# Projecting the values of two head pairs in one call, and moving one small load to another queue

## The chip, the cores and the metric

The kernel runs on one core of a Trainium2 chip. The metric is device microseconds of one execution. A core has engines with instruction streams of their own: PE (TensorE, matrix products), DVE (VectorE), ACT (ScalarE), POOL (GpSimd) and SP (SyncE, which here only issues DMA transfers). Each stream is executed in order; streams wait for one another by semaphores.

## The reference

One decoder layer over 1024 positions of width 1024, in float32:

```
h = rms_norm(x, norm_mix)
xa, ga, q, f, v, g, m_a, m_b = split(h @ w_in)       # eight groups of 1024 columns
y_a = rg_lru(conv(xa)) * gelu(ga)
y_b = rms_norm(hgrn2(silu(q), f, v)) * silu(g)       # 8 heads of 128
x = x + (sigmoid(m_a) * y_a + sigmoid(m_b) * y_b) @ w_out
x = x + relu(rms_norm(x, norm_mlp) @ w_up)**2 @ w_down
out = rms_norm(x, norm_final)
```

The change touches only how `v`, the group of values, is computed from `h`, and how the weights of the first norm (`norm_mix`, a "gain") come in.

## The kernel before

**Precision.** Every float32 matrix is split into a high and a low part in a reduced format: ACT copies the high part (`wH`, `hT0H`), DVE subtracts it to get the low part (`wL`, `hT0L`). `mm3` (lines 113 to 117) then issues three matmuls, one line each: 115 (high times low), 116 (high times high), 117 (low times high). So every product of a 128x128 stationary block with a moving tile is three matmuls.

**Halves and pairs.** The sequence is worked in two halves of 512 positions (`c` = 0, 1). In a half, the eight heads are worked as four pairs (`p` = 0..3), 256 columns of each group at a time. For a pair the program order is: `project_v`, then `project` of xa, convolution, q, f, the RG-LRU (`rg_lru`, products `pr` and `pi`), the HGRN2 recurrence (`hgrn`), and the gates with the projections g, mb, ga, ma (`gates`), which end with transposes `poT`, and with DVE and ACT work on `g`, `sma` and `y` (the tail of the gates). After the four pairs of the first half, `out_proj` multiplies by `w_out`, and `first_norm(1)` for the second half is done between the two column halves of it. The output product of the second half, the second norm and the MLP follow.

**project and project_v.** `project` keeps a block of weights stationary and moves 512 positions of the normed, transposed input `hT`: 48 matmuls of 512 columns for two banks. `project_v` needs the values with positions on the partitions, so it does the reverse: a 128-position block of `hT` is stationary, and weights move, 256 columns (one pair). For each of four row tiles `tt` it issues 8 blocks `k` times three matmuls, 96 in all, and ACT copies each bank into the tile `v` (line 293).

**Weights.** They come as tiles of 128x1024 in the order of the list `seq`, over SP's queue (`load_w`, line 84) into four `raw` buffers. `split_w` makes the high and low parts in a pool of six buffers, so three weight tiles are held at a time; `get_w` prepares up to two tiles ahead of the one in use, and a new one needs the buffers of the tile three before it.

**PSUM banks.** The projections, `project_v` and `out_proj` share four banks (tag `pj`); the transposes use two others (tag `hg`).

**The start.** `first_norm(0)` loads four row tiles of `x` and the first three weight tiles by SP's queue, and the gain (128 rows of 4 KB, the same row for every partition) by ACT's queue (line 130). For each row tile: ACT squares and sums (line 136), DVE and POOL make the reciprocal root, DVE scales (line 139), PE transposes (`xT_x`, line 145), ACT and DVE split the result into `hT0H` and `hT0L`.

**What sets the order.** The programs of the engines are written by a scheduler that follows priorities and its own estimate of when inputs are ready, so instructions of neighbouring steps may be interleaved. In the first norm the order of ACT, DVE and POOL is fixed to that of the program text (`keep`).

Of the kernel before, what the change touches and what calls it, by code (L numbers as in the profile page):

```python
# [18 lines left out]
P = 128  # L19
D = 1024  # L20
# [3 lines left out]
NPAIR = 4  # L24
# [1 line left out]
F_MIN = 1e-30  # L26
GELU_C = 0.7978845608028654
GROUPS = {"xa": 0, "ga": 1, "q": 2, "f": 3, "v": 4, "g": 5, "ma": 6, "mb": 7}
ORDER = ("v", "xa", "q", "f", "rg", "g", "mb", "ga", "ma")
N_PAIR_TILES = 17  # L30
MIX_TILES = NPAIR * N_PAIR_TILES
OUT_TILES = 8
QUADS = 16
LEVELS = (2, 8)

# [6 lines left out]
def trunk(ctx: ExitStack, tc: tile.TileContext, x, wts, mlp, pv, gains, mask_f, mask_u, out):  # L42
    nc = tc.nc
    V, A, G, PE = nc.vector, nc.scalar, nc.gpsimd, nc.tensor
# [13 lines left out]
    def bank(tag, name):  # L58
        return ps.tile([P, 512], F32, tag=tag, name=name, bufs={"pj": 4, "sc": 2, "hg": 2}[tag])


    seq = []
    for c in range(NC):
        seq += list(range(MIX_TILES + OUT_TILES))
    seq += list(range(MIX_TILES, MIX_TILES + OUT_TILES))
    ready, made = {}, [0]

# [41 lines left out]
    def next_w():  # L109
        used[0] += 1  # L110
        return get_w(used[0] - 1)

    def mm3(o, ah, al, bh, bl, first, last, goes_on=False):
        how = {"skip_group_check": True} if goes_on else {}
        PE.matmul(o, ah, bl, start=first, stop=False, **how)  # L115
        PE.matmul(o, ah, bh, start=False, stop=False, **how)  # L116
        PE.matmul(o, al, bh, start=False, stop=last, **how)  # L117
# [7 lines left out]
    mhalf = const.tile([P, 8], F32, tag="mhalf", name="mhalf")  # L125
    G.memset(mhalf, -0.5)

    def gain_tile(i):
        g = const.tile([P, D], F32, tag="gain", name=f"gain{i}", bufs=1)
        nc.scalar.dma_start(g, gains[i : i + 1, :].to_broadcast([P, D]))  # L130
        return g


# [20 lines left out]
    def kt(set_, k):  # L154
        return set_[0][k // 4][:, k % 4, :], set_[1][k // 4][:, k % 4, :]
# [9 lines left out]
    gain0 = []  # L165
# [4 lines left out]
    def mt(tag, name, shape=(P, T), dt=F32, bufs=1):  # L170
        return m.tile(list(shape), dt, tag=tag, name=name, bufs=bufs)
# [59 lines left out]
    hT = []  # L231
# [3 lines left out]
    def first_norm(c):  # L235
        dst = a2_set(a2h, f"hT{c}")
        xts = []
        for tt in range(4):
            r = c * 4 + tt
            xt = mt(X_TAGS[tt], f"x{r}", (P, D)) if c == 0 else tile_x(f"x{r}")  # L240
            nc.sync.dma_start(xt, x[r * P : (r + 1) * P, :])
            xts.append(xt)
            if c == 0 and tt == 0:
                gain0.append(gain_tile(0))
            if c == 0 and tt < 3:
                raws.append(load_w(seq[tt]))
        xns = {}

        def rows(tt):
            xns[tt] = mt("f" if tt % 2 == 0 else "tmp", f"xn{c}{tt}", (P, D))  # L250
            norm_rows(xts[tt], xns[tt], gain0[0], f"x{c}{tt}")

        def weights(n):
            if c == 0:
                fill_w(n)

        rows(0)
        weights(1)
        transposed(xns[0], dst, 0, f"x{c}0")
        rows(1)  # L260
        weights(2)
        for tt in range(1, 4):
            if tt < 3:
                rows(tt + 1)
            transposed(xns[tt], dst, tt, f"x{c}{tt}")
        weights(3)
        in_order[0] = False
        hT.append(dst)
# [10 lines left out]
                    mm3(pp[s], wh[:, cols], wl[:, cols], hh, hl, half == 0 and k == 0, half == 1 and k == 3)  # L279
        return pp  # L280

    def project_v(c, name):
        v = mt("v", f"v_{name}", (P, 4, 256))
        w = [next_w(), next_w()]
        for tt in range(4):
            pp = bank("pj", f"pv_{name}_{tt}")
            for k in range(8):
                hh, hl = kt(hT[c], k)
                cut = slice(tt * P, (tt + 1) * P)
                cols = slice((k % 4) * 256, (k % 4 + 1) * 256)  # L290
                wh, wl = w[k // 4]
                mm3(pp[:, :256], hh[:, cut], hl[:, cut], wh[:, cols], wl[:, cols], k == 0, k == 7)
            A.copy(v[:, tt, :], pp[:, :256])
        return v

    def conv(c, p, pp):
# [84 lines left out]
    def hgrn(c, p, q1, f, kk, v):  # L381
# [43 lines left out]
        for li, cw in enumerate(LEVELS):  # L425
            g = 256 // cw
# [8 lines left out]
            for d, a in ((1, 0), (2, 3), (3, 5)):  # L435
                w = (4 - d) * cw
# [39 lines left out]
        for n in range(8):  # L476
            for b in (0, 2):
                k = 4 * n + b
# [42 lines left out]
        for s in range(2):  # L521
            u = 2 * p + s
            pk = bank("hg", f"pk{c}{u}")
            for n in range(nkv):
                PE.transpose(pk[:, n * P : (n + 1) * P], kk[:, s * T + n * P : s * T + (n + 1) * P], ident)
            kT = mt("kT", f"kT{c}{u}", (P, 4, P))
            A.copy(kT[:, :nkv, :], pk[:, : nkv * P].rearrange("p (n k) -> p n k", n=nkv))
            pkv = bank("hg", f"pkv{c}{u}")
            vn = lambda n: v[:, n, s * P : (s + 1) * P]
            for n in range(nkv):  # L530
                PE.matmul(pkv[:, n * P : (n + 1) * P], kT[:, n, :], vn(n), start=True, stop=True)
            sn = mt("sn", f"sn{c}{u}", (P, 3, P))
            state = lambda n: scar[:, u, :] if n in (0, 4) else sn[:, n - 1, :]
            po = bank("hg", f"po{c}{u}")
            for n in range(4):
                only = c == 0 and n == 0
                on_ps = po[:, n * P : (n + 1) * P]
                PE.matmul(on_ps, scT[:, 4 * s + n, :], vn(n), start=True, stop=only)
                if not only:
                    at = s * T + n * P  # L540
                    PE.matmul(on_ps, qf[:, at : at + P], state(n), start=False, stop=True)  # L541
                if n < nkv:
                    kv = pkv[:, n * P : (n + 1) * P]
                    if only:
                        V.tensor_copy(state(1), kv)
                    else:
                        V.scalar_tensor_tensor(
                            state(n + 1), state(n), t128[:, 4 * s + n : 4 * s + n + 1], kv, op0=ALU.mult, op1=ALU.add
                        )
            for n in range(4):  # L550
                A.activation(  # L551
                    on[:, 4 * s + n, :], po[:, n * P : (n + 1) * P], AF.Square, accum_out=ssq[:, 4 * s + n : 4 * s + n + 1]
                )
            A.copy(on[:, 4 * s : 4 * s + 4, :], po.rearrange("p (n d) -> p n d", n=4))
# [71 lines left out]
    for c in range(NC):  # L626
        if c == 0:
            first_norm(0)
            mu32 = small_inputs()
        else:  # L630
            out_proj(0, ys, res0, done0, lambda: first_norm(1))
        ys = a2_set(a2y, f"y{c}")
        for p in range(NPAIR):
            v = project_v(c, f"{c}{p}")
            px = project(c, f"xa{c}{p}")
            if c == 0 and p == 0:
                parameters()
                tc.keep_in_program_order(V.tensor_copy(mu, mu32.to_broadcast([P, 7, 8, 32])))
            xc3 = conv(c, p, px)
            q1 = q_of(c, p, project(c, f"q{c}{p}"))  # L640
            f, kk = f_of(c, p, project(c, f"f{c}{p}"))
            with tc.high_priority(300):
                h = rg_lru(c, p, *xc3)
            on = hgrn(c, p, q1, f, kk, v)
            gates(c, p, h, on, ys)
# [68 lines left out]
    for part in range(2):  # L714
# [5 lines left out]
        for hf in range(2):  # L720
            pp = {tt: bank("pj", f"po1{hf}{tt}") for tt in tts}
            for j in range(4):
                wh, wl = next_w()
                for k in range(2):
                    ku = 2 * j + k
                    yh, yl = kt(ys, ku)
                    cols = slice(k * 512, (k + 1) * 512)
                    for tt in tts:
                        cut = slice(tt * P, (tt + 1) * P)
                        mm3(pp[tt], yh[:, cut], yl[:, cut], wh[:, cols], wl[:, cols], ku == 0, ku == 7)  # L730
            for tt in tts:
                cols = slice(hf * 512, (hf + 1) * 512)
# [16 lines left out]
    def quad_steps(i, pools, raws=raw_tile):  # L749
# [42 lines left out]
        (q, g): dram.tile([P, 2 * len(g) * T], F32, tag=f"u{q}{g[0]}", name=f"u{q}{g[0]}")  # L792
        for q in range(QUADS - 2)
        for g in U_GROUPS
# [59 lines left out]
    work[0]["b"]()  # L854
    for q in range(QUADS):
        n = q + 1 if q + 1 < QUADS else QUADS + QUADS - 2
        if n > 1:
# [78 lines left out]
    for kb in range(n_kb):  # L936
        last = kb + 1 == n_kb
        qs = order[2 * kb : 2 * kb + 2]
        for half in range(2):
# [8 lines left out]
            for step, (bk, wo, uo), prs in [  # L948
                (i, plan, prs) for prs in ([(pr,) for pr in pairs] if alone else [pairs]) for i, plan in enumerate(PLAN)
            ]:  # L950
                for pr in prs:
# [3 lines left out]
                    cut = slice(pr * P, (pr + 1) * P)  # L955
                    for i, q in enumerate(qs):
                        wh, wl = ops_w[QUADS + q][wo]
                        uh, ul = u_ops[q][uo]
                        mm3(banks[bk, pr], uh[:, cut], ul[:, cut], wh, wl, first and i == 0, i == 1, not first)
                for pr in prs:  # L960
                    _, ci, cj, op = ADDS[step]
# [22 lines left out]
def _weights(w_in, w_r, w_i, w_out):  # L984
    tiles = []
    win = _pairs(w_in)
    for p in range(NPAIR):
        for name in ORDER:
            if name == "rg":
                r = np.concatenate([w_r[p].reshape(2, P, 256), w_i[p].reshape(2, P, 256)])  # L990
                tiles.append(r.transpose(1, 0, 2).reshape(1, P, 1024))
            else:
                tiles.append(win[GROUPS[name] * 4 + p])
    wo = w_out.reshape(4, 2, P, 2, 512).transpose(3, 0, 2, 1, 4)
    tiles.append(wo.reshape(8, P, 1024))
    return np.ascontiguousarray(np.concatenate(tiles))


# [50 lines left out]
```

## Time and profile before

| | |
|---|---|
| three runs | 1618.15, 1622.5, 1622.98 us; median 1622.5 |
| the profiled execution's own time | 1617.3 us |
| its span, first to last instruction | 1615.5 us |
| PE busy | 1571.4 us, 97% of the span, 9240 matmuls |
| DVE / ACT / POOL busy | 1210.2 / 761.5 / 63.8 us |
| granted TensorE clock | 0.996 of full speed |

The page of the profile gives busy times for each engine, the chain of work that ended last, and groups of instructions. Rows of the timeline read: start in microseconds from the span's start, duration, engine, line, operation, output and inputs, partitions and columns, and in brackets how long the engine sat idle before and what it waited for. Durations of matmuls overlap: the next one starts before the last has ended, so the pace of PE is read from start to start.

### The profile page before, as it was taken

To read this page: it belongs to the slowest core of one execution; us is meant where nothing else is said; L and a number is where in the kernel's file an instruction comes from. 1 tells how busy PE (TensorE), PEld (TensorE's weight loads), DVE (VectorE), ACT (ScalarE), POOL (GpSimd) and SP (SyncE) were. 2 spreads that over 40 slices of the span, in tenths; PEclk is the share of its full clock that TensorE was granted. 3 is DMA by queue.
4 is the path that set the end of the run, shared out by engine and by line. 5 is a ranking of instruction groups with operands and counts; after the bars stand their busy time and mean duration, and the time that the engine had idled before them with its cause. 6 is when DMAs were issued, how large, how long until landed. Compare 5 with 4: busy or idle time off the path is not lost.

```text
span 1615.5 us, 23190 instructions
## 1 busy us (share of the span) xinstructions
PE 1571.4 (97%) x9240; PEld 1303.4 (81%) x9240; DVE 1210.2 (75%) x1751; ACT 761.5 (47%) x1186; POOL 63.8 (4%) x99
## 2 busy tenths in 40 slices
PE   7999999999999999999999997999999999999998
PEld 6788788788788788788787876888888878888886
DVE  5975966848763865947758688888888888888876
ACT  4643445436432544446345476677667732122113
POOL 0010000100100000000100000000000000000000
PEclk9999999999999999999999998999999999999999
DMA  6212223222243222222222272666666575666652
GB/s 238 92 66 92 92 66 99 72 92 92 79 167 134 92 66 91 92 68 100 69 92 92 95 245 79 258 245 240 247 258 237 229 279 210 258 258 244 258 218 104
DMA packets 57996, 246.51 MB, mean 153 GB/s; under 512 B 6688, under 2 KB 6816, under 8 KB 47136
## 3 DMA queue, kind: packets, MB, share of 16 engines
q1 hardware_dynamic: 56304, 239.27, 40.5%
q10 hardware_dynamic: 1584, 5.77, 1.0%
q8 instruction: 72, 1.18, 0.3%
q14 instruction: 36, 0.29, 0.1%
HBM read 185.24 MB, written 59.77 MB: 152 GB/s over the span
## 4 chain that ended last, share of the span: by engine, by line
PE 81%; DVE 15%; DMA 1%; issue 1%; ACT 1%; POOL 0%; DVEq 0%; POOLq 0%; SPq 0%
PE dX L115 3%; PE dX L116 3%; PE dX L117 3%; PE uX L115 3%; PE uX L117 3%; PE uX L116 3%; DVE wL L77 2%; PE pj_ga L117 2%; PE pj_ga L116 2%; PE pj_ga L115 2%; PE pj_ma L116 2%; PE pj_ma L117 2%; PE pv L115 2%; PE pv L117 2%; PE pv L116 2%; PE pj_ma L115 2%
## 5 line engine op out<-in xcount | busy, mean ns | idle before, releaser
L77 DVE TENSOR_TENSOR wL<-raw,wH 128x1024 fp32r<-128x1024 f32 x160 | 194.5, 1215 | 151.5 <-ACT wH L76 148.7
L76 ACT CAST wH<-raw 128x1024 fp32r<-128x1024 f32 x160 | 167.9, 1049 | 165.9 <-issue 67.2
L963 DVE TENSOR_TENSOR acc<-acc,dX 128x512 f32<-128x512 f32 x128 | 86.9, 684 | 27.6 <-PE dX L117 27.3
L76 ACT CAST wA<-q 128x512 fp32r<-128x512 f32 x32 | 19.8, 621 | 130.7 <-PE dX L117 80.9
L963 DVE TENSOR_TENSOR acc<-acc,dY 128x512 f32<-128x512 f32 x64 | 43.4, 685 | 14.0 <-PE dY L117 12.8
L345 DVE RECIPROCAL rr<-rr 128x512 f32<-128x512 f32 x16 | 53.5, 3346 | 0.0
L823 ACT ACTIVATE b<-b 128x512 f32<-128x512 f32 x48 | 30.2, 630 | 35.8 <-DVE b L822 35.8
L115 PE MATMUL pv<-wL,hT0H 128*128 128x256 f32 x128 | 37.3, 292 | 0.0
L117 PE MATMUL pv<-wH,hT0L 128*128 128x256 f32 x128 | 37.0, 289 | 0.0
L116 PE MATMUL pv<-wH,hT0H 128*128 128x256 f32 x128 | 36.9, 288 | 0.0
L115 PE MATMUL pv<-wL,hT1H 128*128 128x256 f32 x128 | 36.5, 285 | 0.0
L117 PE MATMUL pv<-wH,hT1L 128*128 128x256 f32 x128 | 36.2, 283 | 0.0
L116 PE MATMUL pv<-wH,hT1H 128*128 128x256 f32 x128 | 36.2, 283 | 0.0
L311 DVE SCALAR_TENSOR_TENSOR xc<-xp,pvt,xc 128x512 f32<-128x512 f32 x48 | 33.1, 747 | 0.0
L551 ACT ACTIVATE on<-po 128x128 f32<-128x128 f32 x64 | 16.9, 278 | 33.5 <-PE po L541 33.2
L570 ACT ACTIVATE smb<-pj_mb 128x512 f32<-128x512 f32 x16 | 9.6, 597 | 45.3 <-PE pj_mb L117 45.1
L824 ACT ACTIVATE b<-b 128x512 f32<-128x512 f32 x48 | 30.0, 630 | 1.1
L565 ACT ACTIVATE g<-pj_g 128x512 f32<-128x512 f32 x16 | 9.6, 599 | 37.3 <-PE pj_g L117 37.3
L384 DVE TENSOR_TENSOR seg<-seg 128x128 f32<-128x128 f32 (+2 forms) x96 | 26.8, 309 | 0.2
L444 POOL TENSOR_SCALAR seg<-seg 128x128 f32<-128x128 f32 (+1 forms) x16 | 12.6, 790 | 360.2 <-DVE seg L384 360.2
L117 PE MATMUL pj_ga<-hT1H,wL 128*128 128x512 f32 x64 | 26.5, 414 | 0.0
L384 DVE TENSOR_TENSOR kk<-kk,seg 128x768 f32<-128x768 f32 (+1 forms) x32 | 26.2, 819 | 0.3 <-DVE dd L438 0.3
(1854 smaller groups left out, 5245.8 us busy)
## 6 DMA issues: line engine op xcount, KB each, us to landing
raw<-wts_in SPq DMA_DIRECT2D x160, 512.0 KB, 3.4
q<-mlp_in SPq DMA_DIRECT2D x64, 512.0 KB, 4.0
x<-x_in SPq DMA_DIRECT2D x8, 512.0 KB, 5.9
acc<-x ACTq DMA_DIRECT2D x8, 512.0 KB, 5.4
y_out<-acc SPq DMA_DIRECT2D x16, 256.0 KB, 2.0
xs<-x_in SPq DMA_DIRECT2D x8, 256.0 KB, 4.3
x<-xs SPq DMA_DIRECT2D x8, 256.0 KB, 2.2
x2s<-x_in SPq DMA_DIRECT2D x4, 512.0 KB, 4.5
```

The source lines that it names most:

```text
L76: keep(A.copy(h, src))
L77: keep(V.tensor_tensor(out=lo, in0=src, in1=h.bitcast(F32), op=ALU.subtract))
L115: PE.matmul(o, ah, bl, start=first, stop=False, **how)
L116: PE.matmul(o, ah, bh, start=False, stop=False, **how)
L117: PE.matmul(o, al, bh, start=False, stop=last, **how)
L311: V.scalar_tensor_tensor(xc[:, s, :], xp[:, j : j + T], pvt[:, PV_CW + 8 * j + u : PV_CW + 8 * j + u + 1], xc[:, s, :], op0=ALU.mult, op1= ...
L345: V.reciprocal(rec, rec)
L384: mul = lambda o, a, b: V.tensor_tensor(out=o, in0=a, in1=b, op=ALU.mult)
L551: A.activation(on[:, 4 * s + n, :], po[:, n * P : (n + 1) * P], AF.Square, accum_out=ssq[:, 4 * s + n : 4 * s + n + 1])
L823: A.activation(b[:, at, :], b[:, at, :], AF.Relu, scale=-1.0 if at == 2 else 1.0)
L824: A.activation(b[:, at, :], b[:, at, :], AF.Square)
L963: V.tensor_tensor(out=dst, in0=dst, in1=banks[bk, pr], op=op)
```

## The change

Values are projected once for two pairs. The value weights leave the order of a pair (17 tiles become 15) and are packed anew: four tiles for the first two pairs and four for the last two, each with two blocks `k` of 512 columns. `seq` puts four of them ahead of pairs 0 and 2 of each half. `project_v` is called for even pairs only. It moves 512 columns and holds all four `pj` banks at once: weight tile by weight tile, and in each all four row tiles. For the very first call (`by_rows`), the first three weight tiles are taken together, and each row tile goes through these three before the next row tile, in the program text; the fourth weight tile comes after. The tile `v` is 512 columns wide instead of 256, and `hgrn` picks its quarter of it. The gain of the first norm is loaded by SP's queue, directly behind the first row tile of `x`, instead of ACT's.

```diff
-ORDER = ("v", "xa", "q", "f", "rg", "g", "mb", "ga", "ma")
-N_PAIR_TILES = 17
+ORDER = ("xa", "q", "f", "rg", "g", "mb", "ga", "ma")
+N_PAIR_TILES = 15
+V_TILES = 4
...
     for c in range(NC):
-        seq += list(range(MIX_TILES + OUT_TILES))
+        for p in range(NPAIR):
+            if p % 2 == 0:
+                at = MIX_TILES + OUT_TILES + p // 2 * V_TILES
+                seq += list(range(at, at + V_TILES))
+            seq += list(range(p * N_PAIR_TILES, (p + 1) * N_PAIR_TILES))
+        seq += list(range(MIX_TILES, MIX_TILES + OUT_TILES))
     seq += list(range(MIX_TILES, MIX_TILES + OUT_TILES))
...
-    def gain_tile(i):
+    def gain_tile(i, queue=nc.scalar):
         g = const.tile([P, D], F32, tag="gain", name=f"gain{i}", bufs=1)
-        nc.scalar.dma_start(g, gains[i : i + 1, :].to_broadcast([P, D]))
+        queue.dma_start(g, gains[i : i + 1, :].to_broadcast([P, D]))
         return g
...
             if c == 0 and tt == 0:
-                gain0.append(gain_tile(0))
+                gain0.append(gain_tile(0, nc.sync))
...
-    def project_v(c, name):
-        v = mt("v", f"v_{name}", (P, 4, 256))
-        w = [next_w(), next_w()]
+    def project_v(c, name, by_rows):
+        v = mt("v", f"v_{name}", (P, 4, 512))
+        pp = [bank("pj", f"pv_{name}_{tt}") for tt in range(4)]
+
+        def product(tt, j, w):
+            cut = slice(tt * P, (tt + 1) * P)
+            for k in (2 * j, 2 * j + 1):
+                hh, hl = kt(hT[c], k)
+                cols = slice(k % 2 * 512, (k % 2 + 1) * 512)
+                mm3(pp[tt], hh[:, cut], hl[:, cut], w[0][:, cols], w[1][:, cols], k == 0, k == 7)
+
+        early = 3 if by_rows else 0
+        w = [next_w() for _ in range(early)]
         for tt in range(4):
-            pp = bank("pj", f"pv_{name}_{tt}")
-            for k in range(8):
-                hh, hl = kt(hT[c], k)
-                cut = slice(tt * P, (tt + 1) * P)
-                cols = slice((k % 4) * 256, (k % 4 + 1) * 256)
-                wh, wl = w[k // 4]
-                mm3(pp[:, :256], hh[:, cut], hl[:, cut], wh[:, cols], wl[:, cols], k == 0, k == 7)
-            A.copy(v[:, tt, :], pp[:, :256])
+            for j in range(early):
+                product(tt, j, w[j])
+        for j in range(early, V_TILES):
+            w = next_w()
+            for tt in range(4):
+                product(tt, j, w)
+        for tt in range(4):
+            A.copy(v[:, tt, :], pp[tt])
         return v
...
-            vn = lambda n: v[:, n, s * P : (s + 1) * P]
+            vn = lambda n: v[:, n, (u % 4) * P : (u % 4 + 1) * P]
...
-            v = project_v(c, f"{c}{p}")
+            if p % 2 == 0:
+                v = project_v(c, f"{c}{p}", c == 0 and p == 0)
...
+    at = GROUPS["v"] * 1024
+    wv = w_in[:, at : at + 1024].reshape(4, 2, P, 2, 512).transpose(3, 0, 2, 1, 4)
+    tiles.append(wv.reshape(8, P, 1024))
```

How the scheduler orders it is seen at three places. (In the names, a weight tile carries its number in the packed weights: the eight new value tiles are 68 to 75; `pv_00_2` is half 0, pair 0, row tile 2, followed by the buffer's own number.)

First, the head of SP's queue, before:

```order
L241 DMA x_110<-x_in 128x1024
L84 DMA raw_114<-wts_in 128x1024
L241 DMA x_116<-x_in 128x1024
L84 DMA raw_118<-wts_in 128x1024
L241 DMA x_120<-x_in 128x1024
L84 DMA raw_122<-wts_in 128x1024
L241 DMA x_124<-x_in 128x1024
```

and of the change:

```order
L247 DMA x_110<-x_in 128x1024
L136 DMA gain_112<-gains_in 128x1024
L90 DMA raw_114<-wts_in 128x1024
L247 DMA x_116<-x_in 128x1024
L90 DMA raw_118<-wts_in 128x1024
L247 DMA x_120<-x_in 128x1024
L90 DMA raw_122<-wts_in 128x1024
L247 DMA x_124<-x_in 128x1024
```

The gain stands second in SP's queue; before, it was the first transfer of ACT's. All else keeps its order.

Second, PE in the first call of the change, where the products with the third weight tile (70) begin; 36 value matmuls and all 32 transposes of the first norm stand ahead of them:

```order
L121 MATMUL pv_00_2_229<-wL69_157,hT0H0_106 128x512
L122 MATMUL pv_00_2_229<-wH69_156,hT0H0_106 128x512
L123 MATMUL pv_00_2_229<-wH69_156,hT0L0_108 128x512
L121 MATMUL pv_00_0_227<-wL70_215,hT0H1_107 128x512
L122 MATMUL pv_00_0_227<-wH70_214,hT0H1_107 128x512
L123 MATMUL pv_00_0_227<-wH70_214,hT0L1_109 128x512
```

Row tiles 0, 1 and 2 first take weight tiles 68 and 69, and tile 70 only then; row tile 3 takes all three afterwards, and the 24 products with tile 71 come last. From the first product with tile 70 to the end of the call, 60 matmuls are left.

Third, PE in the change at the first call of the second half, behind `out_proj`; 18 value matmuls stand ahead of these rows:

```order
L121 MATMUL pv_10_1_4206<-wL69_4157,hT1H0_3968 128x512
L122 MATMUL pv_10_1_4206<-wH69_4156,hT1H0_3968 128x512
L123 MATMUL pv_10_1_4206<-wH69_4156,hT1L0_3970 128x512
L121 MATMUL pv_10_2_4207<-wL68_4127,hT1H0_3968 128x512
L122 MATMUL pv_10_2_4207<-wH68_4126,hT1H0_3968 128x512
L123 MATMUL pv_10_2_4207<-wH68_4126,hT1L0_3970 128x512
```

Row tiles 0 and 1 run ahead with weight tile 69, so that the first matmul of row tile 2 is the 22nd of the call, and that of row tile 3 the 32nd. Before, row tiles 2 and 3 began with the 49th and the 73rd matmul of 256 columns.

Elsewhere the streams of DVE, ACT and PE keep their order, with weight tiles renumbered; behind the second half's mixer DVE and ACT have the same instructions and waits in the same order.

## The prediction

> **What bounds the kernel now.** I read the page first (busy times), then PE's waits, then windows by stage, and at last the timeline where the change acts.
>
> ```profile
> PE 1571.4 (97%) x9240; PEld 1303.4 (81%) x9240; DVE 1210.2 (75%) x1751; ACT 761.5 (47%) x1186; POOL 63.8 (4%) x99
> PE xT_x L145 <- DVE xn L139: 10.3, 2, 9.4
> PE sc L394 <- DVE qb L384: 5.0, 8, 0.6
> 126.17:233.50 107.33, 105.92 (x759) 88.92 (x757) 75.50 (x115) 49.87 (x83) 7.70 (x11) 1.00 0.25 84
> ```
>
> The first row is from the page, the next two are PE's waits (total us, times, longest), the last is a window over exactly one head pair (length; PE, PEld, DVE, ACT, POOL busy; granted clock; DMA share; GB/s). PE is busy 105.92 of 107.33 us of a pair, DVE 75.50. So a pair lasts as long as PE's matmuls take to issue, and a matmul removed from it shortens the run. PE's one long wait is that for the first normed rows, 9.4 us at the start.
>
> **The matmuls: 768 of 256 columns become 384 of 512.** Busy times of overlapping matmuls don't give a price, so I go from start to start. The first two rows are the second and the last matmul of one call of `project_v`, the last two stand 16 triples apart in `out_proj`, whose form is that of the new call: a 128-position block stationary, 512 weight columns moving.
>
> ```profile
> 126.38 0.28 PE L116 MATMUL pv<-wH,hT0H 128*128 128x256 f32 x1
> ...
> 137.65 0.28 PE L117 MATMUL pv<-wH,hT0L 128*128 128x256 f32 x1
> ...
> 483.43 0.39 PE L115 MATMUL po<-wL,y0H 128*128 128x512 f32 x1
> ...
> 494.31 0.39 PE L115 MATMUL po<-wL,y0H 128*128 128x512 f32 x1
> ```
>
> 256 columns: (137.65 - 126.38) / 94 = 0.1199 us. 512 columns: (494.31 - 483.43) / 48 = 0.2267 us. Two short ones take 0.2398 us, so each two that are merged save 0.0131 us. Two old calls take 192 x 0.1199 = 23.02 us, one new call 96 x 0.2267 = 21.76 us: 1.26 us saved. There are four such places; three of them (the second call of the first half and both of the second half) are PE-bound and give 3 x 1.26 = 3.8 us. The first is reckoned below.
>
> The Trainium skill speaks against this price: "TensorE: Matmul & The Clock Gate", section "Back-to-back issue gap", gives columns / 2.4 + 2.5 ns for a warm matmul. By that rule 256 columns take 109.2 ns and 512 take 215.8, and all four places would save only 1.0 us. The rows above show a fixed part five times as large, so the trace does not agree and decides.
>
> **ACT's copies** go from 32 of 256 columns to 16 of 512.
>
> ```profile
> L293 ACT COPY v<-pv 128x256 f32<-128x256 f32 x32 | 11.8, 369 | 29.7 <-PE pv L117 29.7
> L577 ACT COPY g<-pj_ga 128x512 f32<-128x512 f32 x16 | 9.5, 595 | 0.0
> ```
>
> A copy of 512 columns took 0.595 us, so 16 cost 9.5 us in place of 11.8, on an engine busy 47%: nothing on the path. Row tile 0 is finished 18 matmuls (4.1 us) before the call ends, so its bank is copied before xa wants it. Weight tiles and splits stay the same in number (160), hence DVE's load too.
>
> **The start.** These rows follow the first norm and the first call:
>
> ```profile
> 0.71 0.41 ACTq L130 DMA_DIRECT2D gain<-gains_in  x1
> 0.72 5.21 DMA x<-x_in
> gain<-gains_in ACTq DMA_DIRECT2D x1, 512.0 KB, 5.5
> DMA packets 52, 0.21 MB, mean 355 GB/s; under 512 B 0, under 2 KB 0, under 8 KB 52
> q10 hardware_dynamic: 28, 0.11, 62.2%
> q1 hardware_dynamic: 24, 0.10, 45.9%
> 7.47 1.04 ACT L76 CAST wH<-raw 128x1024 fp32r<-128x1024 f32 x1 [0.37 <-DMA raw<-wts_in]
> 8.04 1.28 DVE L139 SCALAR_TENSOR_TENSOR xn<-x,rstd_x,gain 128x1024 f32<-128x1024 f32 x1 [0.75 <-POOL rstd_x L138]
> 9.38 1.97 PE L145 MATMUL xT_x<-ident,xn 128*128 128x128 f32 x8 [9.38 <-DVE xn L139]
> 10.53 0.59 ACT L76 CAST hT0H<-xT_x 128x512 fp32r<-128x512 f32 x1 [2.02 <-PE xT_x L145]
> 11.87 1.06 ACT L136 ACTIVATE xn<-x 128x1024 f32<-128x1024 f32 x1
> 12.71 0.41 PE L117 MATMUL pv<-wH,hT0L 128*128 128x256 f32 x1
> 13.99 0.41 PE L117 MATMUL pv<-wH,hT0L 128*128 128x256 f32 x1
> 25.03 1.23 DVE L77 TENSOR_TENSOR wL<-raw,wH 128x1024 fp32r<-128x1024 f32 x1 [0.26 <-ACT wH L76]
> 29.62 0.40 PE L115 MATMUL pj_xa<-hT0L,wH 128*128 128x512 f32 x1
> ```
>
> The first row tile lands at 0.72 + 5.21 = 5.93 us. The packet rows are for 3.1 to 3.7 us: ACT's queue (q10, the gain) and SP's (q1, the row tile) share the engines half and half. Behind the row tile the gain no longer competes: its 0.52 MB at 355 GB/s take 1.5 us, of which I count 1.4 since it started later. The row tile then lands near 4.5 us. From landing to the scaled rows took 8.04 - 5.93 = 2.11 us, so these begin at 6.65 us. The gain must be there by then: before it landed at 0.71 + 5.5 = 6.2 us with as many bytes ahead of it or beside it, so it is. PE's transposes begin at about 8.0 us.
>
> What follows is less sure, since the first weight tile still comes third (at 7.47 us, by the cast that waited for it). ACT casts it until 8.5, then the two transposed halves (0.59 us each, the second behind PE's 1.97 us of transposes) until 10.5, and squares row tile 1 at 10.5 in place of 11.87: 1.4 us earlier. The order of ACT and DVE up to the third weight tile is fixed and otherwise the same, so that tile's low part, ready at 25.03 + 1.23 = 26.26, is ready at 24.9. PE has 36 matmuls and the transposes to do until then. Its first matmuls are slow: (13.99 - 12.71) / 6 = 0.213 us for 256 columns, so I price the first six at twice that, and the 36 at 6 x 0.43 + 30 x 0.2267 = 9.4 us; with 32 transposes at 1.97 / 8 us or less they fit into the 16.9 us from 8.0 to 24.9. From there 60 matmuls are left, 60 x 0.2267 = 13.6 us, so xa begins at 38.5 us. The fourth weight tile needs the buffers of the first: PE lets these go 24 matmuls (5.4 us) into the 60, and comes to the fourth tile 12 matmuls (2.7 us) later; cast and subtraction (1.04 + 1.23 us) fit.
>
> Before, xa began at 29.62, and the second call, 11.5 us, followed later: 41.1 us by the same count. The start gives 41.1 - 38.5 = **2.6 us**, the first 1.26 included. Bounds: 1.2 if the norm is no earlier (26.26 + 13.6 = 39.9); 3.2 if all of it is 2 us earlier, which is as far as the first weight tile's landing lets it.
>
> **The seam of the halves** is where a wait is added. The four banks are left by `out_proj`, and DVE drains them with a residual:
>
> ```profile
> 496.35 0.28 PE L115 MATMUL pv<-wL,hT1H 128*128 128x256 f32 x1
> 494.51 1.37 DVE L613 TENSOR_TENSOR xs<-po,xs 128x512 f32<-128x512 f32 x2 [1.50 <-PE po L117]
> 500.36 0.69 DVE L613 TENSOR_TENSOR xs<-po,xs 128x512 f32<-128x512 f32 x1 [1.95 <-DMA xs<-x_in]
> 503.14 0.69 DVE L613 TENSOR_TENSOR xs<-po,xs 128x512 f32<-128x512 f32 x1 [2.09 <-DMA xs<-x_in]
> ```
>
> The drains of banks 2 and 3 wait for loads and end at 501.05 and 503.83. The old call came to bank 2 after 48 matmuls (496.35 + 5.8 = 502.1) and to bank 3 after 72 (505.0): no wait. The new one comes to bank 2 after 21 matmuls, 496.35 + 4.8 = 501.1, just in time, and to bank 3 after 31, 503.4: a wait of 0.45 us, I take 0.5. Behind it on PE stands the rest of the call, so it is lost. Bounds: 0, and 2.8 us (503.14 - 500.36, the spacing of the two loads) if they land one place later.
>
> **Odd pairs begin without values**, so the projection of xa follows the transposes of the pair before at once. What was hidden under the value matmuls must fit elsewhere:
>
> ```profile
> 126.17 0.36 PE L115 MATMUL pv<-wL,hT0H 128*128 128x256 f32 x1
> 130.52 1.46 DVE L77 TENSOR_TENSOR y0L<-sma,y0H 128x512 fp32r<-128x512 f32 x2
> 150.96 4.10 DVE L311 SCALAR_TENSOR_TENSOR xc<-xp,pvt,xc 128x512 f32<-128x512 f32 x6
> ```
>
> The tail of the gates ends at 131.98, 5.8 us after the seam at 126.17. DVE's next work with xa, the convolution, comes only after xa's 48 matmuls, 48 x 0.2267 = 10.9 us after the seam. 5.1 us of cover remain, and the weights of xa are split ahead of the tail: cost nothing. Without that cover each odd pair would pay what is late beyond 5.1 us.
>
> **Sum:** 3.8 + 2.6 - 0.5 = 5.9 us. Against the profiled execution, 1617.3 us, that is 1611.4. The runs shown have their median, 1622.5, 5.2 us above it; the mean of the four times (1617.3, 1618.15, 1622.5, 1622.98) is 1620.2. I set 1620 - 6 = **1614 us**.
>
> **Rivals.**
> *The start gives nothing of its own* (1.2 for 2.6): the rows' chain is bound by the first weight tile on ACT (for: ACT's cast waited 0.37 us on it) or PE's slow first matmuls. Sum 4.5, about 1615.5.
> *The residual loads are late by one place*, and PE waits 2.8 us at the seam of the halves. For: DVE waited 1.95 and 2.09 us on them. Against: their order on SP's queue is unchanged. Sum 3.6, about 1616.5.
> *Only columns count:* a merged matmul takes as long as two, and the 0.0131 us don't go, as if they were a matter of streaming and not of each matmul. For: the second call of `project_v` itself has no 512-column row before. Against: the `out_proj` rows, of the same form. Sum 2.6 - 1.26 - 0.5 = 0.8, about 1619. The rule of the Trainium skill quoted above would come out near the same time, 1.0 us from the matmuls and as much from the start.
> *Slower: the lost cover of the odd pairs decides.* Each of the four odd pairs begins with the tail unfinished, the convolution is late, and PE stands at `pr`, which needs its result. It takes a tail of the gates ending 5.1 us later before anything is lost, and 2.7 us more in each of the four pairs before the kernel is slower by 4.9 us (4 x 2.7 = 5.9 + 4.9). With the tail 9 us late: 4 x 3.9 = 15.6 lost, about 1630. Against: DVE is idle for 30% of a pair.
>
> **Chances.** Forecast 0.62; start without gain 0.17; late loads 0.07; columns only 0.07; slower by lost cover 0.07. Faster or slower is counted beyond 0.3%, 4.9 us, about what a measurement of this kernel can tell from no change. The forecast lies only 1 us beyond that, so 0.02 of it and most of the next three fall to "same": faster 0.64, same 0.28, slower 0.08. Range: the best sum is 3.8 + 3.2 = 7.0 and the poorest of the two likeliest kinds 3.8 + 1.2 - 2.8 = 2.2, on a base between 1617.3 and 1623: 1610 to 1621; I give 1608 to 1621.
>
> **What would show it.** Matmuls of `pv` 0.227 us apart, 384 of them; the first scaled rows at 6.7 us, xa's first matmul at 38.5; a wait of PE near 0.5 us on DVE in the first call of the second half; pairs without values 95.8 us long. Wrong would be a new wait of PE at `pr` or at xa in odd pairs, or a gain landing after 6.7 us.

## The result, and the profile after

| | before | changed |
|---|---|---|
| median of 7 runs each, us | 1620.0 (1617.76 to 1622.98) | 1613.83 (1611.92 to 1616.24) |
| ratio, 95% interval | | 0.9963 (0.995 to 0.9976) |
| the profiled execution's own time, us | 1617.3 | 1614.85 |

The change makes the kernel 6.2 us faster (3.9 to 8.1 by the interval); 1614 was predicted. These rows of the changed kernel answer to the first fence of the prediction: the page's PE row, two of PE's waits, and the window over the first pair without values.

```profile
PE 1567.8 (97%) x8856; PEld 1281.7 (79%) x8856; DVE 1209.2 (75%) x1751; ACT 760.2 (47%) x1170; POOL 63.7 (4%) x99
PE xT_x L151 <- DVE xn L145: 8.5, 2, 7.8
PE sc L410 <- DVE qb L400: 4.9, 8, 0.6
134.94:230.79 95.85, 94.40 (x663) 77.41 (x661) 73.04 (x113) 46.45 (x77) 7.69 (x11) 1.00 0.26 83
```

384 matmuls are gone, and the wait for the first normed rows fell from 9.4 to 7.8 us. A pair without values lasts 95.85 us (95.8 was predicted); PE is busy 94.40 of it, so it is still the bound.

Where the time went is read best from PE's starts behind each set of transposes `poT`: there the end of one piece of work and the start of the next can be told apart. The timeline has, for the changed kernel and then for the kernel before, the first matmul of xa (changed kernel only; before it is in the prediction), of the second call of values (changed kernel) or the third (before), of `out_proj`, of the second half's second pair, of the second half's second call of values or its third, and of the output product of the second half, which I call the mixer's end:

```profile
38.42 0.39 PE L121 MATMUL pj_xa<-hT0L,wH 128*128 128x512 f32 x1
230.79 0.48 PE L121 MATMUL pv<-wL,hT0H 128*128 128x512 f32 x1
444.24 0.47 PE L121 MATMUL po<-wL,y0H 128*128 128x512 f32 x1
609.59 0.48 PE L121 MATMUL pj_xa<-hT1L,wH 128*128 128x512 f32 x1
705.50 0.48 PE L121 MATMUL pv<-wL,hT1H 128*128 128x512 f32 x1
918.93 0.48 PE L121 MATMUL po<-wL,y1H 128*128 128x512 f32 x1
```
```profile
233.53 0.36 PE L115 MATMUL pv<-wL,hT0H 128*128 128x256 f32 x1
448.55 0.48 PE L115 MATMUL po<-wL,y0H 128*128 128x512 f32 x1
603.60 0.36 PE L115 MATMUL pv<-wL,hT1H 128*128 128x256 f32 x1
710.97 0.36 PE L115 MATMUL pv<-wL,hT1H 128*128 128x256 f32 x1
925.74 0.47 PE L115 MATMUL po<-wL,y1H 128*128 128x512 f32 x1
```

With two pairs as one block, four gains follow from these starts: 2.74 us to the second pair's end (230.79 against 233.53, where 2.6 was predicted), 1.57 in the second block of the first half (predicted 1.26), then from 444.24 to the middle of the second half (705.50, before 448.55 to 710.97) 1.16 (predicted 1.26 less 0.5), and 1.34 in the last block. The mixer ends 6.81 us earlier; 5.9 was predicted. Of the surplus, 0.4 is in the third block, where the wait that the forecast puts at the seam did not occur, and 0.3 in the second.

The two profiled executions differ by less, 2.4 us in span. Behind the mixer's end the kernel before took 1615.5 - 925.74 = 689.8 us in its profiled execution, the changed one 694.2. That is not the change: the runs below that went back to old values or old widths took 695.0 (only the gain moved) and 694.7 (matmuls split again) there, the other two without extra work in the tail or ahead of the rows 694.3 and 695.7. The execution profiled before was a short one behind the mixer, as its time also says (1617.3 against a median of 1620.0). The mixer's end is therefore the ruler for the experiments, and the median over runs stands beside it. No kernel was profiled twice, so how far that ruler varies was not measured. One hint is the runs with longer tails below: up to xa their PE issues the same matmuls as the changed kernel, and xa's first matmul stands at 38.56 and 39.34, against 38.42. A difference of less than 1 us between single executions shows little.

The start in the changed kernel (timeline; the first column is the start, the last bracket the idle time before and what ended it):

```profile
3.99 1.06 ACT L142 ACTIVATE xn<-x 128x1024 f32<-128x1024 f32 x1 [2.00 <-DMA x<-x_in]
6.42 1.28 DVE L145 SCALAR_TENSOR_TENSOR xn<-x,rstd_x,gain 128x1024 f32<-128x1024 f32 x1 [1.09 <-DMA gain<-gains_in]
7.61 1.05 ACT L82 CAST wH<-raw 128x1024 fp32r<-128x1024 f32 x1 [2.47 <-DMA raw<-wts_in]
7.76 1.97 PE L151 MATMUL xT_x<-ident,xn 128*128 128x128 f32 x8 [7.76 <-DVE xn L145]
10.06 0.77 PE L121 MATMUL pv<-wL,hT0H 128*128 128x512 f32 x1 [0.33 <-DVE wL L83]
10.24 1.06 ACT L142 ACTIVATE xn<-x 128x1024 f32<-128x1024 f32 x1
11.90 0.63 PE L122 MATMUL pv<-wH,hT0H 128*128 128x512 f32 x1
12.33 0.63 PE L123 MATMUL pv<-wH,hT0L 128*128 128x512 f32 x1
23.40 1.22 DVE L83 TENSOR_TENSOR wL<-raw,wH 128x1024 fp32r<-128x1024 f32 x1 [0.26 <-ACT wH L82]
25.02 0.39 PE L122 MATMUL pv<-wH,hT0H 128*128 128x512 f32 x1
38.19 0.39 PE L123 MATMUL pv<-wH,hT0L 128*128 128x512 f32 x1
```

The first square begins at 3.99 (before 5.96), the scaled rows at 6.42, where DVE now waits for the gain, and the transposes at 7.76. The square of row tile 1 is at 10.24, 1.63 us earlier than the 11.87 of before (1.4 was predicted), and the third weight tile's low part is ready at 23.40 + 1.22 = 24.62 (24.9 was predicted). The first six value matmuls are 0.43 us apart (11.90 to 12.33), twice the later distance, and the first eight transposes take 1.97 us (later ones 1.06): below this is called PE's slow pace. The last two rows are 58 matmuls apart, (38.19 - 25.02) / 58 = 0.2271 us each: the price of 0.2267 us holds in the new call.

At the seam of the halves (first matmul of the call, and the drains of banks 2 and 3):

```profile
492.09 0.39 PE L121 MATMUL pv<-wL,hT1H 128*128 128x512 f32 x1
495.91 0.69 DVE L629 TENSOR_TENSOR xs<-po,xs 128x512 f32<-128x512 f32 x1 [1.76 <-DMA xs<-x_in]
498.22 0.69 DVE L629 TENSOR_TENSOR xs<-po,xs 128x512 f32<-128x512 f32 x1 [1.62 <-DMA xs<-x_in]
```

The drains end at 496.60 and 498.91, which is 4.51 and 6.82 us behind the call's start. PE needs the banks 4.8 and 7.03 us behind it: no wait in this execution.

### The profile page after: what moved, and what is told of

Its sections match the earlier page's. It is cut to its first block, busy times and chain, and to the rows that moved or that the text cites. A ratio compares the mean times of both kernels' runs of the same rounds, so it can differ in the third digit from the quotient of the medians.

```text
span 1613.1 us, 22407 instructions
## 1 busy us (share of the span) xinstructions
PE 1567.8 (97%) x8856; PEld 1281.7 (79%) x8856; DVE 1209.2 (75%) x1751; ACT 760.2 (47%) x1170; POOL 63.7 (4%) x99
## 4 chain that ended last, share of the span: by engine, by line
PE 79%; DVE 16%; DMA 2%; issue 1%; ACT 1%; POOL 0%; SPq 0%; DVEq 0%; POOLq 0%; ACTq 0%
PE uX L121 3%; PE uX L123 3%; PE uX L122 3%; PE dX L121 3%; PE dX L122 3%; PE dX L123 3%; DVE wL L83 2%; PE pj_ga L123 2%; PE pj_ga L122 2%; PE pj_ga L121 2%; PE pj_ma L121 2%; PE pj_ma L123 2%; PE pj_ma L122 2%; PE pj_f L123 2%; PE pj_f L121 2%; PE pj_f L122 2%
## 5 line engine op out<-in xcount | busy, mean ns | idle before, releaser
L121 PE MATMUL pv<-wL,hT0H 128*128 128x512 f32 x64 | 26.0, 406 | 0.3 <-DVE wL L83 0.3
L123 PE MATMUL pj_ga<-hT0H,wL 128*128 128x512 f32 x64 | 26.2, 409 | 0.0
L122 PE MATMUL pj_ga<-hT0H,wH 128*128 128x512 f32 x64 | 25.8, 403 | 0.0
L121 PE MATMUL uX<-h2B11L,wA 128*128 128x512 f32 x64 | 25.0, 391 | 0.7 <-DVE rstd_h L143 0.7
L83 DVE TENSOR_TENSOR wA<-q,wA 128x512 fp32r<-128x512 f32 x32 | 21.9, 685 | 4.9 <-ACT wA L82 4.9
L123 PE MATMUL pv<-wH,hT0L 128*128 128x512 f32 x64 | 25.6, 400 | 0.0
```

The costliest lines, as they stand in the source:

```text
L83: keep(V.tensor_tensor(out=lo, in0=src, in1=h.bitcast(F32), op=ALU.subtract))
```

## The experiments

The theory: the shorter issue of 512-column matmuls gives 1.26 us in each of the four calls, 5.0 in all; the gain's move some 1.4; and the lost cover of odd pairs costs nothing.

**Splitting the matmuls again.** The calls stay as changed, but each matmul of 512 columns is issued as two of 256 into the halves of the same bank. This takes the width alone out of the change.

```diff
-                mm3(pp[tt], hh[:, cut], hl[:, cut], w[0][:, cols], w[1][:, cols], k == 0, k == 7)
+                for n in range(2):
+                    o = pp[tt][:, n * 256 : (n + 1) * 256]
+                    cols = slice(k % 2 * 512 + n * 256, k % 2 * 512 + (n + 1) * 256)
+                    mm3(o, hh[:, cut], hl[:, cut], w[0][:, cols], w[1][:, cols], k == 0 and n == 0, k == 7, n == 1)
```

> The changed kernel, with each 512-column value matmul issued as two of 256 columns into the two halves of the same bank: 768 short matmuls again, everything else (calls, banks, weight tiles, the gain's queue) as changed. Theory (a matmul has a fixed part of 0.0131 us, and that is the steady gain): 384 x 0.0131 = 5.0 us come back. The first matmul of the second half's output product, 918.93 us in the changed kernel, moves to 923.5 to 924, and the time to about 1618.5, ratio to before 0.9985 to 1.0. Rival (the gain is from the seating: fewer calls, fewer seams, the start): it stays at 918.9 within 0.5, ratio 0.996.

Measured: median 1620.69 us, ratio to before 0.9994 (0.9985 to 1.0003). The gain is gone. The mixer's end, timeline:

```profile
924.83 0.48 PE L121 MATMUL po<-wL,y1H 128*128 128x512 f32 x1
```

It is 5.90 us later than in the changed kernel; the four blocks lost 1.63, 1.31, 1.63 and 1.33. That is beyond the 923.5 to 924 that were expected: 5.90 / 384 = 0.0154 us for each split. The first block also had PE's slow pace longer (the second set of transposes took 1.81 us, in the changed kernel 1.06), and the third a wait of 0.15 us at the seam; the second and fourth, with neither, lost 1.32 / 96 = 0.0138 us for each split. That the width saves time in the value call itself, and not only in `out_proj`, from whose rows it was taken, is shown. The rival "only columns count" falls. What the fixed part consists of is not shown: each matmul has a weight load of its own (the page counts as many for PEld as for PE), so a split doubles both.

**The gain's move alone**, on the kernel before, and **the change without it**:

```diff
-    def gain_tile(i):
+    def gain_tile(i, queue=nc.scalar):
...
-                gain0.append(gain_tile(0))
+                gain0.append(gain_tile(0, nc.sync))
```
```diff
-                gain0.append(gain_tile(0, nc.sync))
+                gain0.append(gain_tile(0))
```

> The kernel before, with only the gain of the first norm moved to the queue of SP behind the first row tile. Theory: row tile 0 lands about 1.9 us earlier (at 4.0), the norm's chain is 1.6 us earlier, and since PE's value matmuls stand behind it, xa's first matmul moves from 29.62 to 28.0 to 28.4; the first matmul of the second half's output product from 925.74 to 924.2 to 924.5. Time 1.3 to 1.6 us less, ratio 0.999. Rival (the landing of the first weight tile sets the start): 29.6 and 925.7, ratio 1.0.

> The changed kernel, with the gain back on the queue of ACT. Theory: row tile 0 lands at 5.9 us again, the third weight tile is ready 1.6 us later (26.2 instead of 24.6), and with 60 matmuls behind it xa's first matmul moves from 38.42 to 39.9; the first matmul of the second half's output product from 918.93 to 920.4. Rival (PE's own matmuls set the first call, not the rows): 38.4 and 918.9.

Measured: alone, median 1619.59 us, ratio 0.9989 (0.9979 to 0.9998). The rows of xa and of the mixer's end:

```profile
28.19 0.40 PE L115 MATMUL pj_xa<-hT0L,wH 128*128 128x512 f32 x1
924.16 0.47 PE L115 MATMUL po<-wL,y1H 128*128 128x512 f32 x1
```

xa is 1.43 us earlier, the mixer's end 1.58. In the change without the move (one execution, 1617.13 us):

```profile
5.89 1.06 ACT L142 ACTIVATE xn<-x 128x1024 f32<-128x1024 f32 x1 [3.45 <-DMA x<-x_in]
15.24 1.94 PE L151 MATMUL xT_x<-ident,xn 128*128 128x128 f32 x8 [1.20 <-DVE xn L145]
40.27 0.39 PE L121 MATMUL pj_xa<-hT0L,wH 128*128 128x512 f32 x1
921.02 0.47 PE L121 MATMUL po<-wL,y1H 128*128 128x512 f32 x1
```

The first square falls back to 5.89, xa comes 1.85 us later than in the changed kernel and the mixer ends 2.09 us later, where 1.5 was expected for both. Not all of it is the gain's: in this execution PE's slow pace lasted longer, as the second set of transposes shows (1.94 us, in the changed kernel 1.06). The run with the move alone had it too (1.94, before 1.07), so its 1.43 may be too little. Between them the move is worth some 1.4 to 2.1 us, and 1.1 us in the medians (0.3 to 3.4 by the interval). The forecast's 1.4 lies in that range; the rival by which the start gives nothing of its own falls.

**Without the order by row tiles.** The first call takes weight tile by weight tile like the others.

```diff
-                v = project_v(c, f"{c}{p}", c == 0 and p == 0)
+                v = project_v(c, f"{c}{p}", False)
```

> The changed kernel, with the first call going weight tile by weight tile like the others, not by row tiles. Theory (PE is nearly always fed from 14.7 us on, in either order, and the matmuls are the same): xa's first matmul at 38.4 within 0.4 us. Rival (the order by row tiles is what fills PE while rows are still being normed): PE runs dry while it waits for rows, 39.5 us or later.

Measured: 1616.46 us in one execution, xa at 38.24, the mixer's end at 919.05 (38.42 and 918.93 with the order). One execution shows no difference from the order in the program text.

**A longer tail of the gates.** The rival on the lost cover puts a point: a tail that ends more than 5.1 us later costs every odd pair the rest. Twelve multiplications by 1.0 for each of the two blocks of `t` were put ahead of the split of `y`, 24 x 0.343 = 8.2 us of DVE from start to start (about 10 was reckoned), in the changed kernel and in the kernel before:

```diff
             V.tensor_tensor(out=t[:, s, :], in0=t[:, s, :], in1=g2[:, s, :], op=ALU.add)
+            for _ in range(12):
+                V.tensor_scalar(t[:, s, :], t[:, s, :], 1.0, None, op0=ALU.mult)
             split(t[:, s, :], *kt(dst, 2 * p + s))
```

> The changed kernel, with 24 multiplications by 1.0 (0.43 us each, about 10 us of DVE) put into the tail of the gates of every pair, ahead of the split of y. Theory (the cover that odd pairs lost): the tail ends about 16 us after the seam, xa's matmuls cover 10.9 and the q matmuls some 2 us more before PE stands at the first matmul of the RG-LRU; so each of the four odd pairs loses about 3 us, even pairs nothing: the first matmul of the second half's output product moves from 918.93 to about 931 (928 to 935), the time to about 1626. Rival (the cover is not needed, other slack takes the tail): 919 to 920.

> The kernel before, with the same 10 us of DVE in the tail of the gates. Theory: every pair begins with 11.5 us of value matmuls and then xa, so the tail (16 us) ends before the convolution could begin (22 us): the first matmul of the second half's output product stays at 925.7 within 1 us, and the time at 1620. Rival (10 us more of DVE in each pair cost time by themselves): 4 us or more later.

Measured: 1631.41 us with the change, ratio 1.0057 (1.004 to 1.0075); 1637.94 without, ratio 1.0104 (1.0089 to 1.0118). But what was lost was not lost in the odd pairs. Three of the four last 95.5 us (95.8 without the extra work), one 97.1. The loss stands where no pair follows: from `out_proj` to the middle of the second half's first block the changed kernel takes 614.19 - 445.28 = 168.91 us instead of 165.35, and the kernel before 607.46 - 448.63 = 158.83 instead of 155.05; and behind the mixer's end, where both kernels take 708 us instead of 690 to 696 (there PE's waits between 915 and 1100 us sum to 21 us in place of 12 in the changed kernel, with new ones for split weights of the MLP, 3.1 and 2.7 us; the rest was not followed). The change loses 3.85 us to its mixer's end, the kernel before 3.91. So my expectation for the changed kernel (3 us in each odd pair) fell, and so did that for the kernel before, since I had not thought of the seam and of the last pair. The rival's "4 us or more" came near in number for the kernel before (3.91), but not by its reason: its pairs still last 107.4 us. What became of the cover in an odd pair is seen in two rows of the timeline, of the changed kernel and with the longer tail: the low part of xc on DVE, and the first matmul of `pr`, which needs it.

```profile
153.67 1.22 DVE L83 TENSOR_TENSOR xcL<-xc,xcH 128x1024 fp32r<-128x1024 f32 x1
157.96 0.50 PE L121 MATMUL pr<-xcL,wH 128*128 128x512 f32 x1
```
```profile
157.28 1.23 DVE L83 TENSOR_TENSOR xcL<-xc,xcH 128x1024 fp32r<-128x1024 f32 x1 [0.84 <-ACT xcH L82]
160.30 0.50 PE L121 MATMUL pr<-xcL,wH 128*128 128x512 f32 x1
```

In the changed kernel xcL is ready at 154.89, 3.1 us before `pr` takes it: beside the 5.1 us ahead of the convolution there are 3.1 us behind it. With the longer tail xcL is ready 3.6 us later, and `pr` begins 2.3 us later without PE waiting: the scheduler had moved matmuls of f ahead of it, 14 in place of 5. Nor did the whole tail stand ahead of the convolution: its first operation began at 149.55 instead of 148.20, and the last three of the 24 multiplications ran between its operations.

**Twice that tail** (24 for each block, 16.5 us) tells whether there is an end to it.

> The changed kernel with 48 multiplications by 1.0 in the tail of the gates of each pair, 16.5 us of DVE at the 0.343 us from start to start that the 24 showed. By the predicted cover (5.1 us until the convolution, each us beyond it lost in each odd pair): 11.4 us in each of four odd pairs, the first matmul of the second half's output product at about 964. By what the 24 showed (8.2 us of DVE cost an odd pair nothing, since the scheduler puts more of f's matmuls ahead of the RG-LRU's): f has 10.9 us of matmuls to put there, so odd pairs lose 0 to 3 us each, and that first matmul stands at 923 to 935, most of it at the seam of the halves.

> The kernel before with the same 48 multiplications. The tail then ends some 22 us after the seam of two pairs and the convolution may begin 22.5 us after it: by either reckoning pairs lose nothing (107.4 us from seam to seam), the seam of the halves some 8 us, and the first matmul of the second half's output product moves from 925.7 to about 934.

Measured in one execution each: 1650.07 and 1649.03 us. PE's waits in the changed kernel (total us, times, longest) and the mixer's end with it, then that of the kernel before with the same tail:

```profile
PE po L121 <- ACT y1H L82: 9.4, 1, 9.4
PE po L121 <- ACT y0H L82: 5.6, 1, 5.6
PE pr L121 <- DVE xcL L83: 3.5, 4, 0.9
935.66 0.48 PE L121 MATMUL po<-wL,y1H 128*128 128x512 f32 x1
```
```profile
935.32 0.48 PE L115 MATMUL po<-wL,y1H 128*128 128x512 f32 x1
```

Now the wait at `pr` is there, four times, once for each odd pair, 0.9 us each, and these pairs last 97.2 to 97.7 us: 1.3 to 1.8 us lost in each. All 48 matmuls of f now stand ahead of `pr`, so that nothing of f is left to cover the wait. In the kernel before the pairs stay at 107.4 us, as with any tail. The two waits at `po` are the loss at the seam of the halves and at the last pair; both kernels have them (9.4 and 5.7 us without the change). To the mixer's end the changed kernel loses 16.73 us, the other 9.58, and the whole lead of 6.81 us is used up: 935.66 against 935.32 (the 935 of the expectation is just passed). Of the 16.73, 0.92 was lost at the start already, where xa came at 39.34. So the rival mechanism exists, but the tail must be some 16 us longer, not the 7.8 (5.1 + 2.7) of the prediction, before it decides.

**Idle PE at the start.** The changed kernel's first value matmuls are 0.43 us apart (11.90 to 12.33 above), half the pace of later. To see whether that is for want of earlier work, products of the identity with itself, whose result nobody reads, were put on PE ahead of the first rows: 22, and then 12.

```diff
+    warm = ps.tile([P, 512], F32, tag="sc", name="warm", bufs=2)
+    for _ in range(22):
+        PE.matmul(warm[:, 0:P], ident, ident, start=True, stop=True)
```

> The changed kernel, with 22 extra 128-column matmuls of the identity on PE before the first rows are there (about 2.3 to 7.7 us), whose result nobody reads. In the changed kernel the first eight transposes took 1.97 us (later ones 1.06) and the first six value matmuls stood 0.427 us apart (later 0.227). Theory (PE is slow only because it has been idle): with the extra matmuls they take 1.1 us and stand 0.227 us apart, ACT gets the transposed rows up to 0.8 us earlier, and xa's first matmul moves from 38.42 to 37.6 to 38.0. Rival (the rows' chain does not hear of it, the first weight tile sets it): the pace changes but xa's first matmul stays at 38.4. Time: not to be told from the changed kernel.

> As the run with 22 extra matmuls of the identity, with 12 of them: the 22 took 7.82 us, issued as 44, and held the first transposes back to 10.02 us. Theory (PE is slow because it has been idle): 12 end before the first rows are there at 7.76 us, the eight transposes take about 1.1 us instead of 1.97 and the first value matmuls stand 0.227 us apart instead of 0.427; xa's first matmul moves from 38.42 to 37.6 to 38.2. Rival (the rows' chain is set by the landing of the first weight tile, 7.6 us): the pace changes and xa's first matmul stays at 38.4.

Measured: with 22, median 1615.68 us, ratio to before 0.9968 (0.9957 to 0.998). They took 7.82 us and held the transposes up to 10.02, so that xa came at 39.80: a miss, by their number. With 12 (one execution, 1615.32 us), timeline (each of these products is recorded twice):

```profile
2.36 5.49 PE L162 MATMUL warm<-ident 128*128 128x128 f32 x24 [2.36 <-POOL ident masks.py:199]
7.80 1.09 PE L151 MATMUL xT_x<-ident,xn 128*128 128x128 f32 x8
10.14 0.47 PE L121 MATMUL pv<-wL,hT0H 128*128 128x512 f32 x1 [1.25 <-DVE wL L83]
11.21 0.39 PE L122 MATMUL pv<-wH,hT0H 128*128 128x512 f32 x1
11.44 0.40 PE L123 MATMUL pv<-wH,hT0L 128*128 128x512 f32 x1
```

The transposes take 1.09 us instead of 1.97, and the value matmuls are 0.22 to 0.31 us apart from the first on. It helps little: the first of them now waits 1.25 us for the first weight tile's low part and begins at 10.14 (10.06 without), and xa comes at 38.09 instead of 38.42, the mixer's end at 919.43 instead of 918.93 (a wait at the seam, below, used the gain up). In the changed kernel's own execution the start is thus bound by the weight tiles and the chain of the rows, and PE's pace is worth 0.33 us. It can be worth more. The execution with twice the tail kept the slow pace until 18.2 us:

```profile
13.89 1.94 PE L151 MATMUL xT_x<-ident,xn 128*128 128x128 f32 x8 [0.63 <-DVE xn L145]
39.34 0.39 PE L121 MATMUL pj_xa<-hT0L,wH 128*128 128x512 f32 x1
```

Its second set of transposes took 1.94 us instead of 1.06, the rows' chain behind them was late, and xa came 0.92 us later than in the changed kernel (0.21 of that stood already at the first scaled rows).

The run with 22 also shows the wait at the seam of the halves that the changed kernel's own execution lacked. PE's rows:

```profile
498.82 0.50 PE L121 MATMUL pv<-wL,hT1H 128*128 128x512 f32 x1 [0.27 <-DVE xs L633]
501.58 0.50 PE L121 MATMUL pv<-wL,hT1H 128*128 128x512 f32 x1 [0.15 <-DVE xs L633]
```

0.42 us in all. With 12 products it is 0.47 us, with the matmuls split 0.15, with twice the tail 0.7; the changed kernel and the runs without the gain's move, without the order by row tiles and with the longer tail have none. It goes by when the residuals land: in the run with 22 the drains of banks 2 and 3 end 5.13 and 7.89 us behind the call's start, in the changed kernel 4.51 and 6.82.

## Why the prediction was right

- **The price of a matmul** (0.0131 us for each two merged, 1.26 a call) held: 0.2271 us in the new call, and splitting them again cost 0.0138 us each in the two blocks that show nothing else (0.0154 over all, 5.90 us). The formula of the Trainium skill ("TensorE: Matmul & The Clock Gate", section "Back-to-back issue gap") has 2.5 ns of fixed time for each matmul, and by it the split would have cost an estimated 384 x 2.5 ns = 1.0 us. The section gives it for the isolated gap and says that in a stream of weight loads and matmuls both set the spacing; the prediction did not say so. The trace does not agree with the formula, and decides.
- **The start** held in sum (2.6 predicted, 2.74 measured), and for the reason given: with the gain behind it the first row tile comes sooner, and the rows' chain with it. That xa came so near to its forecast (38.42 for 38.5) is in part luck: six slow matmuls were reckoned and six seen, but PE's slow pace lasts longer in some executions, and with twelve slow ones xa came at 39.34. One step was mis-sized without harm: the first square began 1.97 us earlier where 1.4 were reckoned, yet from there the rows wait for the gain (1.09 us on DVE) and ACT for the first weight tile (2.47 us), so that only 1.63 us reached the second row tile. The gain was there at 6.42, ahead of the 6.65 that were reckoned for the scaled rows; but the rows could have been scaled 1.09 us sooner, so that the gain and not the row tile set them.
- **The wait at the seam of the halves** (0.5) was no fixed cost: 0 in the profiled execution, 0.15 to 0.7 us in four of the others. Loads late by a whole place, 2.8 us, did not occur.
- **Odd pairs without cover cost nothing:** right, but the step "each odd pair would pay what is late beyond 5.1 us" failed. There were 3.1 us more behind the convolution, and the scheduler could put matmuls of f ahead of `pr`, up to all 48. 8.2 us of extra tail cost three of the four odd pairs nothing, 16.5 us cost 1.3 to 1.8 us each. The slower rival was priced too steeply by this.
- **ACT's copies** cost 9.4 us (9.5 predicted) off the path.
- **The base.** I took 1620 from four times, and the kernel before has 1620.0 as its median over seven runs; with four times that lay 5.7 us apart, so close a hit is luck. The sum, 5.9, is 6.2 in the medians and 6.81 at the mixer's end. The profiled execution of before (1617.3) would have been a poor base: it was a short one, by 5 us behind the mixer.

## What to carry to other kernels

Where PE is the bound and its matmuls are already back to back, take the price of a matmul from start to start of long rows of the same form, at both widths: here the fixed part, 13 to 15 ns, was worth 5 to 6 us for a merge that leaves the column count as it was. A load that is needed later is better put in the queue behind the one that is needed first, where two queues share the same transfer engines, as they did here. And before you price a lost cover, look behind the next consumer as well: slack there, and work that the scheduler can move ahead, come on top of the cover that you see.

## What the runs showed of the hardware that was not expected

PE's first work runs at half pace. The window 7.5 to 13.5 of the changed kernel, with the granted clock in third place from the end:

```profile
7.50:13.50 6.00, 4.87 (x14) 3.39 (x14) 4.03 (x7) 5.25 (x8) 0.55 (x1) 1.00 1.03 410
```

In it the value matmuls are 0.43 us apart. The 1.00 is no measurement of this: the clock records of this trace begin only 12.94 us into the span, with full speed, and a stretch without a record counts as full. Later in the same trace, where there are records, the column does show the slow pace. PE had waited 5.33 us for the second norm, and eight transposes then took 1.94 us, as at the start (1.97):

```profile
972.10:978.90 6.80, 3.02 (x13) 2.68 (x14) 5.92 (x10) 3.77 (x8) 1.72 (x2) 0.50 0.48 177
975.43 1.94 PE L721 MATMUL xT_h<-ident,xn_h 128*128 128x128 f32 x8 [5.33 <-DVE rstd_h L143]
```

With 5.5 us of unread products ahead of them, at the same time since the start, the first value matmuls are 0.22 to 0.31 us apart, and the clock records begin at 7.80 us. So it is PE's earlier activity that counts, and not the time since the start. How long the slow pace lasts differs between executions: the records begin 3.9 us after PE's first matmul in the run without the order by row tiles (7.78 to 11.68), and 10.3 us after it in the run with twice the tail (7.97 to 18.23), with gaps in PE's work in between. What sets it was not tested. The Trainium skill ("TensorE: Matmul & The Clock Gate", "Part 1: The HAM clock gate") says that an idle array starts at half rate and is let go after about 3.4 us of work; the runs agree in kind, and none was let go sooner.

Two transfers on two queues, issued together, were slower for the one that mattered than both on one queue: the first square went from 5.96 to 3.99 us by moving 0.5 MB from ACT's queue behind the row tile in SP's. The two shared the engines half and half, as the packet rows in the prediction show.
